# The weights of the seven products, moved by 96 bytes inside their tiles

## The chip, the core and the metric

The kernel runs on one core of a Trainium2 chip. The metric is the time of one execution on the device in microseconds (us). The core has a matrix engine (TensorE, PE in the profile, with its weight loads as PEld), a vector engine (VectorE, DVE), a scalar engine (ScalarE, ACT), GpSimd (POOL) and a queue that starts transfers (SyncE, SP). Operands of TensorE lie in SBUF, a memory of 128 partitions; an address here is a byte position inside a partition, the same in all 128.

## The reference

A trunk of two layers on 512 frames of 1024 features, float32. Layer 0 has multi-head latent attention, layer 1 chunked attention with a learned bias on one shared key and value; both have a SwiGLU feed-forward part of width 2816, and a norm before and after each part.

```python
def swiglu(h, w_gate, w_up, w_down):
    return (jax.nn.silu(h @ w_gate) * (h @ w_up)) @ w_down

for layer in range(DEPTH):                       # 2
    h = rms_norm(x, attn_pre_g[layer])
    y = mla_mixer(h, ...) if layer < N_A_LAYERS else chunked_mixer(h, ...)
    x = x + rms_norm(y, attn_post_g[layer])
    h = rms_norm(x, ffn_pre_g[layer])
    f = swiglu(h, ffn_w_gate[layer], ffn_w_up[layer], ffn_w_down[layer])
    x = x + rms_norm(f, ffn_post_g[layer])
```

The change touches `h @ w_gate` and `h @ w_up` alone.

## The kernel before

Every float32 matrix product is made of three matmuls. Weights and activations are each split into a high part (rounded to the matmul's format fp32r) and a low part (what is left), and high x high, low x high and high x low are added up in PSUM. A class `Feed` brings the weights: a transfer of 128 x 1024 floats into a `raw` tile, a cast on ScalarE into `whi` (line 141), and a subtraction on VectorE into `wlo` (line 142). `whi` and `wlo` have three buffers each in the pool `wp`, 4096 bytes a partition. `Feed.split` (lines 210 to 239) takes the tiles and hands out a function `at`, from which the matmuls get their 128-column pieces.

Of the 22 blocks of 128 hidden columns, 4 are done whole with matmuls of 512 columns (lines 257 to 260); the other 18 go in 9 pairs a layer through `products` (lines 1038 to 1084). There the 2 x 2 block product of (gate, up) weights with two halves of the activations is made with seven products in place of eight, from sums of weights and of activations. The class `Pair` loads the four blocks of weights of a pair and forms the sums on VectorE (line 171); such weights are those of the plan whose `src` is a `Pair`. One pair is 7 products x 2 output blocks x 4 steps of the contraction x 3 = 168 matmuls at line 1064, each with 128 x 128 weights (`whi` or `wlo`) and 256 moving columns (`th`, `tl`, `xh`, `xl`). They add into PSUM tiles `be`, `al` and `ga`, in the order be, al, ga, al, al, al, be; so the chain shows 48, 24, 24 and 72 in a row. ScalarE and VectorE take the results out (lines 1068 to 1083). Each of the seven weights is used for 24 matmuls.

Where things lie: the pools follow each other in SBUF, and tiles in them without gaps. The small constants end so that all large tiles start at 64 past a multiple of 128 bytes, and even at 192 past a multiple of 512; pieces are cut at multiples of 512 bytes. So in each fp32r matmul of the kernel before, weights and moving operand start at the same place of a 512-byte stretch. Exceptions are the identity (at 0 past a multiple of 128), which is the moving operand of the transposes, and single columns of small tiles of 32 bytes, which line 371 spreads over 128 columns and which start at many multiples of 4.

Of the kernel before, what the change touches and what calls it, by code (L numbers as in the profile page):

```python
# [11 lines left out]
F32R = mybir.dt.float32r  # L12
# [6 lines left out]
D, S, P = 1024, 512, 128  # L19
# [49 lines left out]
def trunk(ctx: ExitStack, tc: tile.TileContext, a, out):  # L69
# [4 lines left out]
    wp = ctx.enter_context(tc.tile_pool(name="wp", bufs=1))  # L74
# [7 lines left out]
    def name_(n):  # L82
        uid[0] += 1
        return f"{n}_{uid[0]}"

    def U(dt=F32, name="u"):
        return up.tile([P, S], dt, tag="u", name=name_(name), bufs=NU)
# [52 lines left out]
    def split(dst_hi, dst_lo, src):  # L140
        return (nc.scalar.copy(dst_hi, src),  # L141
                V.tensor_tensor(dst_lo, src, dst_hi.bitcast(F32), op=OP.subtract))  # L142
# [41 lines left out]
    class Feed:  # L184
# [25 lines left out]
        def split(self, i):  # L210
            while len(self.ready) <= min(i, len(self.plan) - 1):
                j = len(self.ready)
                self.load(j + 2)
                raw, (src, n, gain, room) = self.raw[j], self.plan[j]
                for f in range(j, min(j + 5, len(self.plan))):
                    self.load(f) if isinstance(self.plan[f][0], Pair) else None
                if isinstance(src, Pair):
                    src.sums(gain)
                    raw = src.raw[gain]
                elif gain is not None:  # L220
                    rv = raw[:, :n].rearrange("p (a b) -> p a b", a=gain.shape[1])
                    V.tensor_tensor(rv, rv, gain, op=OP.mult)
                if room is None:
                    pieces = [tuple(wp.tile([P, 1024], F32R, tag=t, name=name_("w" + t), bufs=3) for t in ("hi", "lo"))]
                else:
                    pieces = self.room[room]()
                w = pieces[0][0].shape[1]
                for c in range(0, n, w):
                    m = min(w, n - c)
                    with ExitStack() as st:  # L230
                        for b in self.behind.get(j, ()):
                            st.enter_context(tc.issue_after(b.ins))
                        split(pieces[c // w][0][:, :m], pieces[c // w][1][:, :m], raw[:, c:c + m])

                def at(c, m, pieces=pieces, w=w):
                    o = c % w
                    return tuple(t[:, o:o + m] for t in pieces[c // w])

                self.ready.append(at)
# [142 lines left out]
    class Head:  # L382
# [19 lines left out]
        def turn(self, qt):  # L402
            if self.pt is None:
                self.pt = [pool[0].tile([P, NQT, S], F32R, tag=t, name=name_(t), bufs=n)
                           for t, n in (("pth", 2), ("ptl", 1))]
            n = P * (qt + 1)
            p = self.p.pop(qt)
            t = bank("t", "pt")
            for kt in range(qt + 1):
                nc.tensor.transpose(t[:, kt * P:(kt + 1) * P], p[:, kt * P:(kt + 1) * P], ident)  # L410
            tv = t[:, :n].rearrange("p (a b) -> p a b", b=P)
            q_ = slice(qt * P, (qt + 1) * P)
            split(self.pt[0][:, :qt + 1, q_], self.pt[1][:, :qt + 1, q_], tv)
# [154 lines left out]
    class Split:  # L568
# [5 lines left out]
        def each(self, k, h):  # L574
            c = HALF[h]
            if len(self.xs) <= k:
                self.xs.append((U(F32R, "xh"), U(F32R, "xl")))
            t = cut(self.xs[k], c)
            if self.gain is None:
                split(*t, self.x[k][:, c])  # L580
            else:
                split_scaled(*t, self.x[k][:, c], g(self.gain, k))
# [87 lines left out]
    for k in range(KT):  # L670
        h, l = U(F32R, "xh"), U(F32R, "xl")
        w = feed.next(384, False)
# [14 lines left out]
    for j in range(2):  # L687
        t = U(name="ckv")
# [49 lines left out]
    for j in range(2):  # L738
        V.tensor_tensor(ckv[j], ckv[j], rkv, op=OP.mult)
        h, l = U(F32R, "ckh"), U(F32R, "ckl")  # L740
        feed.behind[13] = feed.behind[14] = split(h, l, ckv[j])
        cks.append((h, l))
# [484 lines left out]
    for kc in range(4):  # L1227
        w = feed.next(1024)
# [111 lines left out]
```

## Time and profile before

| | |
|---|---|
| median of 3 runs | 1162.41 us (1161.83 to 1162.87) |
| the profiled execution | 1162.01 us, span from first to last instruction 1159.9 us |
| TensorE matmuls | busy 98% of the span |
| VectorE | busy 71% |
| ScalarE | busy 53% |
| granted TensorE clock, mean | 0.997 of full speed |

Busy times of matmuls overlap, since a matmul is recorded from its start to the end of its results; their pace is read from the distance of their starts. A time line rounds starts to 0.01 us.

### The profile page before, as it was taken

How to read it: one execution, taken by the hardware profiler on the slowest of the kernel's cores; microseconds unless marked ns; L12 is line 12 of the kernel's file. 1: busy time of each engine (PE TensorE's matmuls, PEld its weight loads, DVE VectorE, ACT ScalarE, POOL GpSimd, SP SyncE). 2: the span in 40 equal slices, each digit the busy share in tenths (PEclk: the TensorE clock that was granted, in tenths of full speed). 3: DMA queues.
4: the chain of work that ended last, by engine and by line, in shares of the span. 5: the costliest groups of instructions: out<-in, count | busy, mean ns of one | idle time of the engine just before them, and what ended most of it. 6: DMA issues, size and time to landing. Idle time of an engine off the chain costs nothing.

```text
span 1159.9 us, 18693 instructions
## 1 busy us (share of the span) xinstructions
PE 1137.9 (98%) x7195; PEld 1018.7 (88%) x7195; DVE 828.8 (71%) x1429; ACT 613.9 (53%) x1159; POOL 29.5 (3%) x51
## 2 busy tenths in 40 slices
PE   9999999999999999999999999999999999999996
PEld 6788889899999998889788887789899999998886
DVE  7787648999898862246968877748998998852233
ACT  6476646656565542224436766656655565632220
POOL 1200000000000000000100000000000000000002
PEclk9999999999999999999999999999999999999998
DMA  7333144323333253233456656454223233252212
GB/s 231 117 113 91 37 149 160 109 79 105 109 92 127 74 170 103 96 118 96 159 158 159 172 152 164 128 176 138 87 92 114 90 108 109 73 189 89 91 50 73
DMA packets 53161, 137.71 MB, mean 119 GB/s; under 512 B 7184, under 2 KB 10768, under 8 KB 53072
## 3 DMA queue, kind: packets, MB, share of 16 engines
q1 hardware_dynamic: 52928, 136.47, 37.6%
q8 instruction: 57, 0.93, 0.3%
q14 instruction: 32, 0.26, 0.1%
q10 hardware_dynamic: 144, 0.04, 0.0%
HBM read 113.22 MB, written 8.59 MB: 105 GB/s over the span
## 4 chain that ended last, share of the span: by engine, by line
PE 85%; DVE 7%; ACT 3%; issue 2%; DMA 2%; POOL 1%; SPq 0%; DVEq 0%; ACTq 0%; POOLq 0%
PE al L1064 16%; PE b L258 16%; PE b L259 16%; PE b L260 16%; PE be L1064 8%; PE ga L1064 4%; PE pt L410 2%; DVE wlo L142 1%; DVE acc L328 1%; POOL r L354 1%; DMA raw<-in_w_pair 1%; ACT whi L141 1%; PE b L1189 1%; PE bc L371 1%; PE b L1190 1%
## 5 line engine op out<-in xcount | busy, mean ns | idle before, releaser
L142 DVE TENSOR_TENSOR wlo<-raw,whi 128x1024 fp32r<-128x1024 f32 (+4 forms) x240 | 278.8, 1162 | 199.0 <-ACT whi L141 197.3
L141 ACT CAST whi<-raw 128x1024 fp32r<-128x1024 f32 (+4 forms) x240 | 240.7, 1003 | 337.8 <-PE b L259 180.6
L258 PE MATMUL b<-hh,whi 128*128 128x512 f32 (+1 forms) x364 | 136.0, 374 | 0.0
L259 PE MATMUL b<-hl,whi 128*128 128x512 f32 (+1 forms) x364 | 135.7, 373 | 0.0
L260 PE MATMUL b<-hh,wlo 128*128 128x512 f32 (+1 forms) x364 | 135.6, 373 | 0.0
L1064 PE MATMUL al<-th,whi 128*128 128x256 f32 x432 | 124.2, 288 | 0.6 <-DVE ut L1076 0.3
L1064 PE MATMUL al<-tl,whi 128*128 128x256 f32 x432 | 122.1, 283 | 0.0
L1064 PE MATMUL al<-th,wlo 128*128 128x256 f32 x432 | 122.1, 283 | 0.0
L258 PE MATMUL b<-xh,whi 128*128 128x512 f32 (+1 forms) x304 | 115.7, 383 | 0.8 <-ACT xh L145 0.8
L259 PE MATMUL b<-xl,whi 128*128 128x512 f32 (+1 forms) x304 | 113.1, 372 | 0.0
L260 PE MATMUL b<-xh,wlo 128*128 128x512 f32 (+1 forms) x304 | 112.8, 371 | 0.0
L171 DVE TENSOR_TENSOR raw<-raw,raw 128x1024 f32<-128x1024 f32 x72 | 86.6, 1218 | 1.1 <-DMA raw<-in_w_pair 0.9
L1064 PEld LDWEIGHTS al<-th,whi 128*128 128x128 f32 x432 | 82.7, 191 | 2.9 <-DVE ut L1076 0.8
L1064 PEld LDWEIGHTS al<-th,wlo 128*128 128x128 f32 x432 | 82.7, 192 | 0.0
L1064 PEld LDWEIGHTS al<-tl,whi 128*128 128x128 f32 x432 | 82.7, 191 | 0.0
L259 PEld LDWEIGHTS b<-hl,whi 128*128 128x128 f32 x364 | 68.5, 188 | 12.0
L258 PEld LDWEIGHTS b<-hh,whi 128*128 128x128 f32 x364 | 68.5, 188 | 12.0
L260 PEld LDWEIGHTS b<-hh,wlo 128*128 128x128 f32 x364 | 68.5, 188 | 11.9
L398 ACT ACTIVATE p<-p,mn 128x128 f32<-128x128 f32 (+1 forms) x96 | 54.0, 562 | 31.9 <-DVE mn L396 31.2
L142 DVE TENSOR_TENSOR ptl<-pt,pth 128x128 fp32r<-128x128 f32 (+1 forms) x96 | 46.3, 485 | 28.8 <-ACT pth L141 23.0
L328 DVE TENSOR_TENSOR acc<-acc,sq 128x256 f32<-128x256 f32 (+1 forms) x89 | 43.3, 505 | 32.1 <-ACT sq L327 31.3
L258 PEld LDWEIGHTS b<-xh,whi 128*128 128x128 f32 x304 | 57.4, 189 | 9.0 <-ACT xh L145 2.1
(266 smaller groups left out, 2831.0 us busy)
## 6 DMA issues: line engine op xcount, KB each, us to landing
raw<-in_w_pair SPq DMA_DIRECT2D x72, 512.0 KB, 3.8
raw<-in_w_down SPq DMA_DIRECT2D x38, 512.0 KB, 3.4
raw<-in_w_o SPq DMA_DIRECT2D x16, 512.0 KB, 3.6
raw<-in_w_gu SPq DMA_DIRECT2D x16, 512.0 KB, 3.7
raw<-in_w_qkb SPq DMA_DIRECT2D x16, 512.0 KB, 3.6
x<-in_x SPq DMA_DIRECT2D x16, 256.0 KB, 5.8
mid<-x SPq DMA_DIRECT2D x16, 256.0 KB, 2.2
x<-mid SPq DMA_DIRECT2D x16, 256.0 KB, 6.2
```

The source lines that it names most:

```text
L141: return (nc.scalar.copy(dst_hi, src), V.tensor_tensor(dst_lo, src, dst_hi.bitcast(F32), op=OP.subtract))
L142: V.tensor_tensor(dst_lo, src, dst_hi.bitcast(F32), op=OP.subtract))
L171: V.tensor_tensor(t, x, y, op=OP.add)
L258: nc.tensor.matmul(o, l[0], r[0], start=start, stop=False)
L259: nc.tensor.matmul(o, l[0], r[1], start=False, stop=False)
L260: nc.tensor.matmul(o, l[1], r[0], start=False, stop=stop)
L328: V.tensor_tensor(self.acc[:, c], self.acc[:, c], q[:, c], op=OP.add)
L354: nc.gpsimd.tensor_tensor(r, v, mhalf[:, :m], op=OP.pow)
L371: nc.tensor.transpose(b[:, (first + i) * P:(first + i + 1) * P], col[:, i:i + 1].to_broadcast([P, P]), ident)
L398: nc.scalar.activation(p[:, :n], p[:, :n], AF.Exp, bias=mn[:, :1], scale=-1.0, accum_out=self.sums[:, qt:qt + 1])
L410: nc.tensor.transpose(t[:, kt * P:(kt + 1) * P], p[:, kt * P:(kt + 1) * P], ident)
L1064: nc.tensor.matmul(o, l[c], r[d], start=first_ and n == 0, stop=k == K2 - 1 and n == 2, skip_group_check=True)
```

## The change

Tiles `whi` and `wlo` get 1056 in place of 1024 elements, 4224 bytes. For weights of a `Pair` the slice that is written and read begins at element 24, that is at byte 96, and 64 + 96 = 160 is 32 past a multiple of 128. All other weights begin at byte 0 of the wider tile.

```diff
@@ -221,7 +221,9 @@
                 if room is None:
-                    pieces = [tuple(wp.tile([P, 1024], F32R, tag=t, name=name_("w" + t), bufs=3) for t in ("hi", "lo"))]
+                    o = 24 if isinstance(src, Pair) else 0
+                    pieces = [tuple(wp.tile([P, 1056], F32R, tag=t, name=name_("w" + t), bufs=3)[:, o:o + 1024]
+                                    for t in ("hi", "lo"))]
                 else:
                     pieces = self.room[room]()
```

The lists of instructions of all engines stay the same, row for row. 3024 of the matmuls, all at line 1064, have their weights at 32 past a multiple of 128 afterwards and their moving operand at 64, as before. All other operands stay where they were past a multiple of 128. Counted from a multiple of 512 more moves: buffers of `whi` and `wlo` are now 4224 bytes apart, and the pools behind `wp` (the small tiles and the tiles of each attention and feed-forward part) begin 768 bytes later.

## Rows read from the trace of the kernel before

**Rows 1.** Page, parts 1 and 2: busy time and share; TensorE's clock.
```profile
PE 1137.9 (98%) x7195; PEld 1018.7 (88%) x7195; DVE 828.8 (71%) x1429; ACT 613.9 (53%) x1159; POOL 29.5 (3%) x51
...
PEclk9999999999999999999999999999999999999998
```

**Rows 2.** Page, part 4: the chain that ended last, by line.
```profile
PE al L1064 16%; PE b L258 16%; PE b L259 16%; PE b L260 16%; PE be L1064 8%; PE ga L1064 4%; PE pt L410 2%; DVE wlo L142 1%; DVE acc L328 1%; POOL r L354 1%; DMA raw<-in_w_pair 1%; ACT whi L141 1%; PE b L1189 1%; PE bc L371 1%; PE b L1190 1%
```

**Rows 3.** The chain in order of time, product stages: start, duration in us, what.
```profile
254.77 1.70 PE al L1064 x12
...
262.24 2.88 PE al L1064 x24
...
419.22 2.88 PE be L1064 x24
...
861.07 1.70 PE al L1064 x12
...
1025.22 2.88 PE be L1064 x24
```

**Rows 4.** Windows of both product stages, line 1064 alone: length, busy (instructions).
```profile
254.77:422.10 167.33, 167.13 (x1380) 166.02 (x1380) 1.00 0.30 97
861.07:1028.10 167.03, 167.03 (x1380) 166.02 (x1380) 1.00 0.31 97
```

**Rows 5.** Time line in a product: start, duration in us, engine, line, instruction.
```profile
270.11 0.28 PE L1064 MATMUL al<-tl,whi 128*128 128x256 f32 x1
270.12 0.19 PEld L1064 LDWEIGHTS al<-th,wlo 128*128 128x128 f32 x1
270.23 0.28 PE L1064 MATMUL al<-th,wlo 128*128 128x256 f32 x1
...
270.35 0.28 PE L1064 MATMUL al<-th,whi 128*128 128x256 f32 x1
270.36 0.19 PEld L1064 LDWEIGHTS al<-tl,whi 128*128 128x128 f32 x1
270.47 0.28 PE L1064 MATMUL al<-tl,whi 128*128 128x256 f32 x1
```

**Rows 6.** Time line in the down projection, 512 moving columns; between them two matmuls.
```profile
500.17 0.39 PE L258 MATMUL b<-hh,whi 128*128 128x512 f32 x1
...
500.85 0.39 PE L258 MATMUL b<-hh,whi 128*128 128x512 f32 x1
```

**Rows 7.** Line 371's loads (min/median/max ns), then the time line behind its last.
```profile
L371 PEld LDWEIGHTS bc<-ident,r x32: 132/136/138, 30.5 to 1151.4; 128*128 128x128 f32 x32
...
31.24 0.14 PEld L371 LDWEIGHTS bc<-ident,r 128*128 128x128 f32 x1
...
31.35 0.19 PEld L258 LDWEIGHTS b<-xh,whi 128*128 128x128 f32 x1
...
31.46 0.19 PEld L259 LDWEIGHTS b<-xl,whi 128*128 128x128 f32 x1
```

**Rows 8.** One pair: window (PE, PEld, DVE, ACT busy); groups of splits in it.
```profile
322.00:342.31 20.31, 20.31 (x171) 20.21 (x170) 18.32 (x24) 11.92 (x20) 0.00 (x0) 1.00 0.34 104
...
L142 DVE TENSOR_TENSOR wlo<-raw,whi 128x1024 fp32r<-128x1024 f32 x7 | 8.6, 1221 | 2.0 <-ACT whi L141 2.0
...
L141 ACT CAST whi<-raw 128x1024 fp32r<-128x1024 f32 x7 | 7.4, 1050 | 6.8 <-PE al L1064 3.6 <-PE be L1064 1.8 <-issue 1.4
```

**Rows 9.** Time line in the attention of layer 1, 512 columns; some matmuls left out.
```profile
611.25 0.40 PE L258 MATMUL b<-xh,whi 128*128 128x512 f32 x1
...
611.48 0.40 PE L259 MATMUL b<-xl,whi 128*128 128x512 f32 x1
611.48 0.19 PEld L260 LDWEIGHTS b<-xh,wlo 128*128 128x128 f32 x1
...
611.72 0.39 PE L260 MATMUL b<-xh,wlo 128*128 128x512 f32 x1
...
612.41 0.39 PE L260 MATMUL b<-xh,wlo 128*128 128x512 f32 x1
```

## The prediction

> **What bounds the kernel now.** I read the page first, then the chain that ended last, then the matmuls one by one. TensorE is busy for 1137.9 of 1159.9 us, and its clock row holds nines to the last slice but one: it runs at the higher of its two levels, 2.4 GHz [rows 1]. The chain spends 16% of the span on the `al` products, 8% on `be` and 4% on `ga`, together 28%, and next to nothing on VectorE, ScalarE or DMA [rows 2]. So the pace of the matmuls sets the time, and the change touches only the matmuls of line 1064.
>
> There are 2 layers x 9 pairs x 168 = 3024 of these. In the chain they run from 254.77 to 422.10 us in layer 0 and from 861.07 to 1028.10 us in layer 1 [rows 3], 334.4 us in all. The view by windows shows PE busy 334.16 of 334.36 us in them [rows 4]. The stage waits for nobody; only a change of the matmul's own pace can shorten it.
>
> That pace: in the run without a wait, matmul starts stand at 270.11, 270.23, 270.35, 270.47 us, so 0.120 us each, and 24 in a row take 2.88 us [rows 3, 5]. The weight loads stand just behind them, at 270.12 and 270.36 us: the load for the next matmul begins when the present one begins, so weights and moving columns are read at the same time. Compare 512 columns: from 500.17 to 500.85 us three matmuls pass, 0.2267 us each [rows 6]. The difference, 0.1067 us for 256 more columns, is 0.417 ns a column, one column per cycle at 2.4 GHz. Hence 256 columns alone would take 106.7 ns, and each matmul, short or long, carries 13.3 ns beyond its columns. The whole question is what these 13.3 ns are: over 3024 products they make 40 us.
>
> **The change part by part.** No instruction is added, removed or moved; every engine has the same list in the same order, the same waits, the same DMAs. Three things differ, all of them addresses.
>
> (1) The products' weights are read from 32 past a multiple of 128 instead of 64, while the moving operand stays at 64. The trace of before can't price this directly: there both operands of all these fp32r matmuls start at the same place of a 128-byte stretch. I bound it. Below: weight loads of the identity transposes, which have the shortest matmuls, follow each other in 0.11 us (31.24, 31.35, 31.46 us) [rows 7]. So at best the pace falls from 120 to 110 ns, 3024 x 10 ns = 30 us. VectorE sets nearly the same floor: in one pair it is busy 18.32 of 20.31 us [rows 8], so not more than 2.0 us a pair, 36 us over 18 pairs, could come out. Above: the same 512-column matmul also runs slower than 226.7 ns. After two score matmuls of another length, six of them start from 611.25 to 612.41 us, five steps of 0.232 us, though the loads stand beside the matmuls as before (the one at 611.48 us, too) [rows 9]; single steps there are 0.24. That is +5 ns (the mean) to some +10 ns (a step of 0.24, 0.01 us above 0.23), so +16 to +30 us over 3024.
>
> What speaks for a value between these ends? The nearest rows on the address of stationary operands are the loads of line 371. Their sources are single columns of small tiles that lie at many places (0, 4, 32, 36, 64, 72, 96, 100 and others past a multiple of 128), and 32 of them took 132 to 138 ns [rows 7]; no place stands out. They read one word again and again, 128 times, and run beside 128 columns that lie at 0, so they are a weak witness. Then there are the 13.3 ns themselves, equal at 256 and 512 columns: a price per matmul, as a swap of weights would be, or as one more stretch of the moving operand would be, fits without any help of the weights' address. I take 0 for this term, and keep -30 and +30 us for the range.
>
> The Trainium skill has a rule that bears on it: "TensorE: Matmul & The Clock Gate", section "Step-by-step: what each phase is for", says that TensorE reads moving and stationary operands through two independent ports, and that loading the next weights takes no read bandwidth from the running matmul. By it this term is 0 whatever the addresses, and the time stays. The 0.232 us of [rows 9], with the same columns and the same loads as the 0.2267, are not explained by it, so I do not rest on it.
>
> (2) ScalarE and VectorE write the high and low parts to the shifted place: 7 casts of 1050 ns and 7 subtractions of 1221 ns a pair [rows 8]. No row has such a write elsewhere. It is hidden: VectorE idles 20.31 - 18.32 = 2.0 us a pair and ScalarE 8.4 us, and three buffers of each tag let the split run ahead of the matmuls. A write dearer by 10% would add 7 x 0.12 = 0.85 us a pair, within the 2.0. Without that cover it would cost 18 x 0.85 = 15 us. I take 0. The first split of each stage lies ahead of the first product without such cover, two times 0.1 us at most.
>
> (3) The padded tiles push the other weights in these buffers, and the pools behind them, by multiples of 128 bytes. These operands stay at 64 past a multiple of 128. If a coarser stretch than 128 bytes mattered, the 512-column matmuls would feel it too; no row shows or excludes that. I take 0, and let the same two bounds stand for it.
>
> Sum: 0. The profiled execution took 1162.0 us for a span of 1159.9, with 2.1 us around it; the median of the runs is 1162.4. Forecast 1162.4.
>
> **The rivals.**
> *The change does nothing measurable* (my forecast): 1162.4, within 0.2%, which is about 2.3 us and what a measurement of this kernel can tell from no change. For it: the constant excess at both lengths, whichever of `th`, `tl`, `xh`, `xl` moves and whether `whi` or `wlo` is loaded; and that the stage runs in perfect step.
>
> *The two reads disturb each other less.* If the 13.3 ns come from the load and the stream getting in each other's way because both begin at the same place of a 128-byte stretch at the same moment, a shift by 32 bytes can relieve that. For it: loads and matmuls start within 0.01 us of each other in every row [rows 5], and the excess is not strictly fixed [rows 9]. Against it: the stream moves twice as fast as the load (512 bytes of weights in 110 ns, 1024 of columns in 107), so it passes the load's place again and again whatever the start. The best is -30 us, 1132; half of it, taken as the middle of nothing and all, is -15 us, 1147. Below 18.3 us a pair VectorE would be the new bound.
>
> *The two reads disturb each other more.* The lock in which the products run, 120.0 ns again and again, is broken, and they run as the 512-column matmuls do at 611 us: +5.3 ns each, 1162.4 + 16 = 1178, up to 1192. It decides as soon as a product takes over 0.8 ns more than now, since 3024 x 0.8 ns is 2.4 us. For it: [rows 9] show that such a slower step exists with nothing late. Against it: those rows are a stream just disturbed, and the down projection settles at 226.7.
>
> *A new wait on VectorE or ScalarE*, because writes at the shifted place are dear: up to 15 us by part (2) if they grew by far more than 10%. I give it a few in a hundred and count it with slower.
>
> That the shift doesn't take place is no rival: the offset of 24 elements is added to the slice that both the split and the matmuls use.
>
> **How the numbers follow.** I give no measurable effect 0.40, less disturbance 0.36, more disturbance (with the new wait) 0.24. The explanations of the excess that leave the weights' address out are simplest, but the trace holds no fp32r product with the two operands at different places, so it doesn't weaken the other two much; and of these I hold the gain for somewhat likelier, since both operands beginning together looks more like an unlucky place than a lucky one. Predicted time: 1162.4, its own range 1160 to 1165. The range for 8 in 10 reaches to 1140 below, which leaves out about 0.12 of gains above three quarters of the bound, and to 1178 above, which leaves out some 0.08.
>
> **What the profile of the changed kernel would show.** Right: products still 0.12 us apart, 2.88 us for 24, a pair at 20.31 us; stages of 167 us; splits at 1050 and 1221 ns. Wrong towards faster: 24 products in 2.6 to 2.8 us, and VectorE above 18.3 of a shorter pair, perhaps with waits for `wlo`. Wrong towards slower: 24 products in 3.0 us, or starts that no longer repeat. If the stages keep their length but the down projection (0.2267 us a step) changes, part (3) was the mistake. If `wlo` or `whi` takes longer and PE waits for it, part (2) was.

## The result and the profile after

The changed kernel takes 1165.14 us (median of 12 runs, 1163.81 to 1166.31) against 1162.45 us (12 runs): ratio 1.0022, interval 1.0013 to 1.0030. It is slower by 2.7 us, 0.22%, and that is more than its measurement is uncertain. The forecast was no measurable change, 1162.4 us, with 1160 to 1165 as its own range.

That small sum hides two larger parts of opposite sign. First the page after: its busy times, and the chain by line.

```profile
span 1164.3 us, 18693 instructions
...
PE 1140.8 (98%) x7195; PEld 1014.9 (87%) x7195; DVE 828.9 (71%) x1429; ACT 614.2 (53%) x1159; POOL 29.5 (3%) x51
...
PE b L261 16%; PE al L1066 16%; PE b L260 16%; PE b L262 16%; PE be L1066 8%; PE ga L1066 4%; PE pt L412 2%; DVE wlo L142 2%; DVE acc L330 1%; ACT whi L141 1%; POOL r L356 1%; DMA raw<-in_w_pair 1%; PE bc L373 1%; PE b L1191 1%; PE b L1192 1%
```

The page looks the same as before; the shift is below its percentages. (Lines past 224 are two further down: line 1066 is the products, 260 to 262 the other matmuls.) The chain in order of time shows the first part: start, duration, what.

```profile
256.16 1.69 PE al L1066 x12
257.85 5.67 PE be L1066 x48
263.52 2.86 PE al L1066 x24
266.38 2.84 PE ga L1066 x24
269.22 8.67 PE al L1066 x72
...
865.14 1.68 PE al L1066 x12
...
1027.06 2.84 PE be L1066 x24
```

Groups of 24 products take 2.84 to 2.86 us where [rows 3] had 2.88. So the products became faster. The stretch of [rows 3] now runs in layer 1 from 865.14 to 1029.90, 164.8 in place of 167.0 us. (The stretches of [rows 3] hold 2 x 1380 of the 3024 products; each stage begins some 16 us earlier, with products that wait in between. The two whole stages took 183.4 and 183.3 us, now 181.1 and 180.9, so -4.7 us.)

The second part is in the down projection, whose weights were not given the offset. Time line after, line 260 to 262, 512 moving columns:

```profile
469.84 0.39 PE L260 MATMUL b<-hh,whi 128*128 128x512 f32 x1
470.06 0.40 PE L261 MATMUL b<-hl,whi 128*128 128x512 f32 x1
470.30 0.40 PE L262 MATMUL b<-hh,wlo 128*128 128x512 f32 x1
470.53 0.39 PE L260 MATMUL b<-hh,whi 128*128 128x512 f32 x1
470.76 0.40 PE L261 MATMUL b<-hl,whi 128*128 128x512 f32 x1
470.99 0.40 PE L262 MATMUL b<-hh,wlo 128*128 128x512 f32 x1
471.23 0.39 PE L260 MATMUL b<-hh,whi 128*128 128x512 f32 x1
```

Six matmuls take 1.39 us, 0.232 us each; in [rows 6] it was 0.2267. In the unrounded starts most groups of three have one step of about 0.227 and two of 0.233 and 0.234.

To add this up I took from the traces the distance from each matmul's start to the next start, wherever it is less than the time of the columns at one per 2.4 GHz cycle plus 32 ns in both traces (longer ones were left out as waits). The products' mean went from 119.92 to 118.16 ns; that of the 924 matmuls of 512 columns in the down projection from 226.73 to 231.94 ns, +4.8 us; that of the some 1260 others of 512 columns from 229.25 to 231.69 ns, +3.1 us. With -4.7 us from the product stages that is +3.2. A wait for a transfer in the attention of layer 1, 0.9 us, and small ones make the rest of the 4.4 us by which the span grew. This execution, 1166.31 us, is the slowest of the 12, so the medians differ by less.

The splits didn't change. Groups of one pair after (320 to 340.1 us):

```profile
L142 DVE TENSOR_TENSOR wlo<-raw,whi 128x1024 fp32r<-128x1024 f32 x8 | 9.8, 1220 | 1.7 <-ACT whi L141 1.6
...
L141 ACT CAST whi<-raw 128x1024 fp32r<-128x1024 f32 x7 | 7.4, 1052 | 6.5 <-PE al L1066 3.6 <-PE be L1066 1.5 <-issue 1.4
```

1220 and 1052 ns stand against 1221 and 1050 in [rows 8]: writing to the other place costs nothing here.

### The profile page after: what moved, and what is told of

It reads as the page before. It is cut to its first block, busy times and chain, and to the rows that moved or that the text cites. A ratio compares the mean times of both kernels' runs of the same rounds, so it can differ in the third digit from the quotient of the medians.

```text
span 1164.3 us, 18693 instructions
## 1 busy us (share of the span) xinstructions
PE 1140.8 (98%) x7195; PEld 1014.9 (87%) x7195; DVE 828.9 (71%) x1429; ACT 614.2 (53%) x1159; POOL 29.5 (3%) x51
## 4 chain that ended last, share of the span: by engine, by line
PE 84%; DVE 8%; ACT 3%; issue 2%; DMA 2%; POOL 1%; SPq 0%; ACTq 0%; DVEq 0%; POOLq 0%
PE b L261 16%; PE al L1066 16%; PE b L260 16%; PE b L262 16%; PE be L1066 8%; PE ga L1066 4%; PE pt L412 2%; DVE wlo L142 2%; DVE acc L330 1%; ACT whi L141 1%; POOL r L356 1%; DMA raw<-in_w_pair 1%; PE bc L373 1%; PE b L1191 1%; PE b L1192 1%
## 5 line engine op out<-in xcount | busy, mean ns | idle before, releaser
L141 ACT CAST whi<-raw 128x1024 fp32r<-128x1024 f32 (+4 forms) x240 | 240.6, 1003 | 340.1 <-PE b L261 185.7
L262 PE MATMUL b<-hh,wlo 128*128 128x512 f32 (+1 forms) x364 | 138.1, 379 | 0.0
```

What stands on the lines that cost most here:

```text
L141: return (nc.scalar.copy(dst_hi, src), V.tensor_tensor(dst_lo, src, dst_hi.bitcast(F32), op=OP.subtract))
L262: nc.tensor.matmul(o, l[1], r[0], start=False, stop=stop)
```

## The experiments

Two theories at first. **Theory A**: the weights of the next matmul are loaded while the present one reads its moving columns, and the pace depends on where the two start against each other in some stretch of addresses. **Theory B**: it depends on whether successive loads start alike. The rows above fit both: with buffers 4224 bytes apart, some of the high and low buffers now differ by 128 bytes from each other and from the moving operands. In the expectations below, theory A first counts places in 128 bytes, as the change's own words do, and in later runs in 256.

All paces, worked out from the traces as above, in ns (products; 512 columns in the down projection; other matmuls of 512 columns). The place is that of the loaded weights minus that of the moving operand, past a multiple of 256 bytes:

| kernel | place: products | place: others | products | down | other 512 |
|---|---|---|---|---|---|
| before | 0 | 0 | 119.92 | 226.73 | 229.25 |
| the change | 96 and 224 | 0 and 128 | 118.16 | 231.94 | 231.69 |
| e1_pad | 0 and 128 | 0 and 128 | 118.79 | 231.94 | 231.76 |
| e2_all96 | 96 | 96 | 117.78 | 234.27 | 233.18 |
| e3_lo128 | high 0, low 128 | the same | 119.11 | 231.17 | 231.13 |
| e4_all128 | 128 | 128 | 118.68 | 232.37 | 232.20 |
| e5_both | 96 and 224 | 0 | 118.23 | 226.74 | 229.28 |
| e6_all256 | 0 (256 further) | 0 (256 further) | 119.92 | 226.73 | 229.34 |
| e7_all64 | 64 | 64 | 114.68 | 233.32 | 232.88 |
| e8_all32 | 32 | 32 | 118.32 | 233.34 | 232.69 |
| e9_only64 | 64 | 0 | 114.74 | 226.73 | 229.37 |
| e10_only192 | 192 | 0 | 117.78 | 226.69 | 229.36 |
| e11_shift | 0 (all operands 64 further) | 0 | 119.92 | 226.73 | 229.14 |
| e12_only16 | 16 | 0 | 118.32 | 226.77 | 229.30 |

**e1_pad: the wide tiles without the offset.**

```diff
-                    pieces = [tuple(wp.tile([P, 1024], F32R, tag=t, name=name_("w" + t), bufs=3) for t in ("hi", "lo"))]
+                    pieces = [tuple(wp.tile([P, 1056], F32R, tag=t, name=name_("w" + t), bufs=3)[:, :1024]
+                                    for t in ("hi", "lo"))]
```

> The wider tiles alone: 4224 bytes each, but all weights begin at byte 0, so the products' weights stay at 64 past a multiple of 128. Theory A (a matmul's pace follows from where the weights loaded beside it lie against its moving operand, counted in 128 bytes): the products return to 120 ns, the matmuls of 512 columns stay as slow as in the changed kernel (231.8 ns in the mean, +7.9 us), so about 1170 us. Theory B (the pace follows from whether successive weight loads begin at the same place of some longer stretch; if all are alike the stream locks at 13.3 ns beyond its columns, wherever they lie): buffers still differ by 128 bytes, so the products run near 118 ns as in the changed kernel, the rest too, and the time is about 1165 us.

1167.14 us against 1162.63, ratio 1.0039 (1.0026 to 1.0051). The matmuls of 512 columns are as slow as in the changed kernel, 231.94 ns: the padding does that, not the offset. The products stay near 119: theory A in 128 bytes had them back at 120 and the time at 1170, theory B at 118 and 1165, and neither is met. A distance of 128 bytes is no harmless one. The offset itself, the change against this kernel, is worth 118.79 - 118.16 = 0.6 ns a product, 1.9 us: it lowers the price of the padding.

**e2_all96, e3_lo128, e4_all128: tiles of 4096 bytes, but gaps of unused bytes ahead of, between and behind the high and low buffers.**

```diff
+    def gap(tag, n):
+        if n and tag not in gone:
+            gone.add(tag)
+            wp.tile([P, n], F32, tag=tag, name=name_("gap"), bufs=1)
...
-                    pieces = [tuple(wp.tile([P, 1024], F32R, tag=t, name=name_("w" + t), bufs=3) for t in ("hi", "lo"))]
+                    pieces = [(gap("ga", A) or tile_w("hi"), gap("gb", B) or tile_w("lo"))]
+                    gap("gc", C)
```

A, B, C in elements are 24, 0, 104; then 0, 32, 96; then 32, 0, 96. What lies behind keeps its place in a stretch of 512 bytes.

> Tiles of 4096 bytes as before, but a gap of 96 bytes ahead of the buffers of high and low parts and one of 416 bytes behind them: all weights that pass through these buffers, the products' and the others, begin at 288 past a multiple of 512, everything else at 192 as before. Theory A: the products run at about 118 ns as in the changed kernel (-5 us), since their place against the moving operand is the same, and the matmuls of 512 columns move one way or the other: 1157 us if these keep their pace. Theory B: all loads are alike again, so 120.0 and 226.7 ns everywhere and 1162.4 us.

> Tiles of 4096 bytes, with 128 bytes between the high and the low buffers and 384 behind them: high parts at 192 past a multiple of 512 as before, low parts at 320, all else as before. Theory B: in each group of three matmuls the load changes place twice, so the down projection shows the cycle 227, 233, 234 ns of the changed kernel, the products run near 118 to 119 ns, and the time is about 1165 us, though no operand has left 64 past a multiple of 128. Theory A counted in 128 bytes: nothing changes, 1162.4 us. Theory A counted in 256 or 512 bytes: only the matmul beside which a low part is loaded is slower, 227, 233, 227, about 1163 to 1165 us.

> Tiles of 4096 bytes, a gap of 128 bytes ahead of the high and low buffers, 384 behind them: all these weights at 320 past a multiple of 512, their moving operands at 192. Theory A counted in 256 or 512 bytes: each load lies 128 bytes away from the moving operand, as in the slow steps of the changed kernel, so matmuls of 512 columns run at 232 to 234 ns: +10 to +15 us, 1172 to 1177 us. Theory B: all loads are alike, 120.0 and 226.7 ns, 1162.4 us.

e2: 1168.06 us, 1.0047 (1.0035 to 1.0060). e3: 1166.36, 1.0033 (1.0021 to 1.0046). e4: 1167.42, 1.0045 (1.0032 to 1.0057). In e2 and e4 all loads start alike, and theory B asked for 120.0 and 226.7 ns; it measured 117.8 and 234.3, 118.7 and 232.4. Theory B falls. Theory A in 128 bytes falls with e3 and e4, where nothing should have changed. In 256 or 512 bytes it had the down projection of e4 rightly at 232 to 234 ns; the time stayed some 5 us below the lower end of the expected 1172 to 1177, since the products gained and the matmuls of 512 columns ran at the lower end. In e2, with every load at the same place, the down projection runs like this:

```profile
472.10 0.40 PE L269 MATMUL b<-hh,whi 128*128 128x512 f32 x1
472.33 0.40 PE L270 MATMUL b<-hl,whi 128*128 128x512 f32 x1
472.56 0.39 PE L271 MATMUL b<-hh,wlo 128*128 128x512 f32 x1
472.80 0.39 PE L269 MATMUL b<-hh,whi 128*128 128x512 f32 x1
473.03 0.40 PE L270 MATMUL b<-hl,whi 128*128 128x512 f32 x1
473.27 0.40 PE L271 MATMUL b<-hh,wlo 128*128 128x512 f32 x1
```

Five steps take 1.17 us, 0.234 each, and nothing waits in between. e3 goes against theory A in part. Counted in 256 bytes it had 227, 233, 227 ns and 1163 to 1165 us; the cycle came as theory B had it, and the time is 1166.4. Time line of e3:

```profile
472.13 0.40 PE L270 MATMUL b<-hl,whi 128*128 128x512 f32 x1
472.36 0.40 PE L271 MATMUL b<-hh,wlo 128*128 128x512 f32 x1
472.60 0.39 PE L269 MATMUL b<-hh,whi 128*128 128x512 f32 x1
472.82 0.40 PE L270 MATMUL b<-hl,whi 128*128 128x512 f32 x1
```

In the mean over the down projection, a step whose own weights and whose loaded weights both lie at the equal place takes 226.9 ns. The step beside which a low part is loaded takes 232.4 ns. The next one, which uses that low part, takes 234.2 ns though a high part at the equal place is loaded beside it. So one load at another place is followed by two slow steps. Theory A is right in that the place counts, and wrong in that only the matmul beside the load pays; why the second one does is open.

**e5_both: the products as in the change, the other weights put back against their moving operands.**

```diff
-                    o = 24 if isinstance(src, Pair) else 0
+                    i = next(turn)
...
-                                    for t in ("hi", "lo"))]
+                                    for t, o in (("hi", 24 if isinstance(src, Pair) else (0, 32, 0)[i]),
+                                                 ("lo", 24 if isinstance(src, Pair) else (32, 0, 32)[i])))]
...
+    slots = "021" * 9 + "012" * 31 + "010" + "210" * 8 + "120" * 31
+    turn = map(int, slots)
```

`turn` says which of the three buffers comes next. In this kernel some instructions also stand in another order: three matmuls in the first stage, and a tenth or so of the places in the lists of ScalarE and VectorE.

> The changed kernel, with the products' weights at byte 96 as there, but every other weight moved by 0 or 128 bytes inside its wide tile, by a table of the buffers' order, so that it starts at 192 past a multiple of 256, as its moving operand does. Theory A, counted in 256 bytes (the pace follows from the place of the loaded weights against the moving operand; equal places lock at 13.3 ns beyond the columns): the products keep 118.2 ns (-5 us), the matmuls of 512 columns are back at 226.7 ns, and the time is about 1157.5 us. If the stretch is 512 bytes: the down projection stays slow (its moving operands are at 448 past a multiple of 512), about 1162 us. Theory C (the products are faster only because successive loads vary): also 1157 us; this run doesn't tell A from C.

1160.41 us against 1162.69, 0.9981 (0.9972 to 0.9990): faster than both kernels. The down projection is back at 226.74 ns though its moving operands lie at 448 past a multiple of 512 and part of the weights at 192, so the stretch is 256 bytes, not 512. Theory C had fallen with e2 already, where all loads start alike and the products run at 117.8 ns. The paces of e5 are as expected, the time is 3 us above it. Its profiled execution loses 3.3 us in the first 16 us of the kernel against the profile of before. TensorE idles there for 2.62 us ahead of 10.10 us, waiting for `xh` (0.79 us before), and from 11.2 to 14.6 us its granted clock is 0.5, the 1.2 GHz level, with 0.43 us a matmul in place of 0.23. The two product stages give -4.1 in place of -5. Whether the other runs lose at the start as well is not shown.

**e6_all256, e7_all64, e8_all32: gaps as in e2**, of 64, 16 and 8 elements ahead (256, 64 and 32 bytes) and 64, 112 and 120 behind.

> Tiles of 4096 bytes, all high and low parts 256 bytes further (448 past a multiple of 512), everything else as before. Theory A counted in 256 bytes: nothing changes, 120.0 and 226.7 ns, 1162.4 us. Counted in 512 bytes: as with 128 bytes, down projection at 232 ns or more and products near 118 to 119, 1167 us.

> As before, all high and low parts 64 bytes further. Theory A, graded: with 96 bytes products ran at 117.8 and the down projection at 234.3 ns, with 128 bytes at 118.7 and 232.4; 64 bytes give some third pair of numbers. Theory A, in which any place but the equal one is alike: products 118 to 119, down projection 232 to 234, about 1167 us.

> As before, all high and low parts 32 bytes further. If the lock needs exactly equal places: 118 to 119 and 232 to 234 ns, about 1167 us. If it only needs the places to lie within some tens of bytes: 120.0 and 226.7 ns, 1162.4 us.

e6: 1162.76 us, 1.0000 (0.9991 to 1.0009), 119.92 and 226.73 ns: 256 bytes are like none. e8, a single run: 1167.7 us, 118.3 and 233.3 ns; 32 bytes already end the equality. e7, a single run: 1160.9 us, where one form of theory A had 1167, and a surprise. The products at 64 bytes, time line of e7:

```profile
301.80 0.28 PE L1075 MATMUL be<-th,whi 128*128 128x256 f32 x1
301.91 0.28 PE L1075 MATMUL be<-tl,whi 128*128 128x256 f32 x1
302.02 0.28 PE L1075 MATMUL be<-th,wlo 128*128 128x256 f32 x1
302.14 0.28 PE L1075 MATMUL be<-th,whi 128*128 128x256 f32 x1
302.25 0.28 PE L1075 MATMUL be<-tl,whi 128*128 128x256 f32 x1
302.37 0.28 PE L1075 MATMUL be<-th,wlo 128*128 128x256 f32 x1
302.48 0.28 PE L1075 MATMUL be<-th,whi 128*128 128x256 f32 x1
302.59 0.28 PE L1075 MATMUL be<-tl,whi 128*128 128x256 f32 x1
```

Seven steps in 0.79 us: 113 ns each, again a stream in step, with 6.7 ns beyond the 106.7 of its columns, half of the 13.3. The matmuls of 512 columns pay as at the other places (233.3 ns). Matmuls of 256 columns in other stages gain, too: those with weights from the same buffers take 115.3 to 118.1 ns by groups (119.2 to 120.0 before), while those with weights from other tiles (`wh`, `wu`) stay at 119.3 to 120.1 ns in every run.

**e9_only64, e10_only192: 64 bytes further, or 64 bytes less (192), for the products alone.** Tiles of 4352 bytes keep all buffers alike past a multiple of 256.

```diff
-                    pieces = [tuple(wp.tile([P, 1024], F32R, tag=t, name=name_("w" + t), bufs=3) for t in ("hi", "lo"))]
+                    o = 16 if isinstance(src, Pair) else 0
+                    pieces = [tuple(wp.tile([P, 1088], F32R, tag=t, name=name_("w" + t), bufs=3)[:, o:o + 1024]
+                                    for t in ("hi", "lo"))]
...
-    nc = bacc.Bacc("TRN2", target_bir_lowering=False, num_devices=1, dynamic_dma_scratch_size=1024)
+    nc = bacc.Bacc("TRN2", target_bir_lowering=False, num_devices=1, dynamic_dma_scratch_size=768)
```

In e10 the 16 is a 48.

> Tiles of 4352 bytes (17 times 256), so that all buffers keep the same place in a stretch of 256 bytes; the products' weights begin at byte 64, all others at byte 0; the memory for it comes from a scratch area made 256 bytes smaller. Theory A (places counted in 256 bytes, equal places lock at 13.3 ns beyond the columns, +64 locks products at 6.7 ns): products at 113.3 to 114.7 ns as with all weights at +64 (-15 us in the stream, some 4 us given back to waits for VectorE), matmuls of 512 columns at 226.7 ns in the down projection, time about 1150 to 1152 us. If the rival that the products only gain from what the other matmuls do beside them (order of buffers, waits) were right, they would fall back to 118 to 120 ns and the time would be 1157 to 1162 us.

> The same with the products' weights at byte 192, that is 64 bytes before the place of the moving operand instead of behind it. If only the distance counts: 113 to 115 ns and about 1151 us. If the side counts, as a race of two reads at different speeds would have it: another pace, between 115 and 122 ns, 1155 to 1165 us.

e9: 1155.75 us against 1162.3, 0.9945 (0.9932 to 0.9959), the fastest of all. Products 114.74, down projection 226.73 ns, as expected; the products do not fall back to 118 to 120, so the rival in its expectation is out. The time lies 4 us above the expected 1150 to 1152. Its five runs spread from 1150.39 to 1157.82 us, more than those of the other kernels. The chain of the profiled (and fastest) run shows what bounds it:

```profile
268.10 8.55 PE al L1066 x72
276.64 5.44 PE be L1066 x48
282.08 2.72 PE al L1066 x24
284.80 2.72 PE ga L1066 x24
287.52 2.73 PE al L1066 x24
...
290.49 1.06 ACT whi L141
...
291.57 1.23 DVE wlo L142
...
293.05 1.22 DVE raw L171
...
307.99 4.63 DMA raw<-in_w_pair
```

24 products take 2.72 us, 113.3 ns each. But from 290 us the chain passes through the split, the sums and a transfer: the weights now come late. The window from 269.91 to 287.52 us of this kernel (PE, PEld, DVE, ACT busy) shows how full VectorE is:

```profile
269.91:287.52 17.61, 17.61 (x154) 17.40 (x154) 16.43 (x21) 10.43 (x18) 0.00 (x0) 1.00 0.28 93
```

VectorE is busy 16.43 of 17.61 us, 93%, where it was 90% in [rows 8]. A supply that runs without room turns each late transfer into waiting, which may be why the runs spread; that was not tried.

e10, a single run: 1157.0 us, products 117.78 ns. The side counts: +64 and -64 are not the same.

**e11_shift: everything moved together by 64 bytes.**

```diff
+    consts.tile([P, 16], F32, name="gap")
```

> The kernel before with a gap of 64 bytes behind the constants, so that all large tiles, weights and moving operands alike, begin at a multiple of 256; their place against each other stays equal. In all runs so far the moving operands lay at 192 past a multiple of 256, so the place of the weights alone (their address) and their place against the moving operand could not be told apart. Theory A (against the moving operand): equal places lock at 13.3 ns, 120.0 and 226.7 ns, 1162.4 us. Theory D (the address of the weights alone): weights at 0 past a multiple of 256, as with +64 before, so products near 114 ns and the down projection at 233 ns, about 1161 us in sum, by the paces plainly different.

1161.77 us, 0.9992 (0.9983 to 1.0002); 119.92 and 226.73 ns. In all runs before this one the moving operands lay at one place, so the address of the weights alone could have been the cause. Here the weights lie where e7 and e9 have them, at 0 past a multiple of 256, and the products take their old 2.88 us for 24. Time line of e11's chain:

```profile
262.00 2.88 PE al L1066 x24
264.88 2.88 PE ga L1066 x24
267.76 8.79 PE al L1066 x72
```

So the address of the weights alone does not decide. In e11 every large tile moved, though, and in the other runs the moving operand of these streams kept its place. The traces hold the opposite case as well: in the value projections (lines 779 and 1102) tiles `whi` and `wlo` are the moving operand, and the loaded weights (`ckh`, `xh` and their low parts) lie in a pool ahead of them, which stays where it was in e2. Time lines of before, then of e2:

```profile
597.86 0.39 PE L258 MATMUL b<-whi,xh 128*128 128x512 f32 x1
...
599.90 0.39 PE L258 MATMUL b<-whi,xh 128*128 128x512 f32 x1
```

```profile
601.64 0.39 PE L269 MATMUL b<-whi,xh 128*128 128x512 f32 x1
...
603.75 0.39 PE L269 MATMUL b<-whi,xh 128*128 128x512 f32 x1
```

Nine steps take 2.04 us before and 2.11 in e2. The mean of these streams (183 steps) is 233.4 ns in e2, 232.9 in e4, 232.6 in e7 and 233.3 in e8, against 227.0 to 227.1 before, in e6 and in e11. Moving the weights alone changes the pace, so does moving the moving operand alone, and moving both by the same distance doesn't: the place of the two against each other decides.

**e12_only16: the products' weights 16 bytes further** (o = 4 in e9).

> As the kernel with only the products' weights at +64, but with these at +16 bytes. If the lock needs equal places to the byte or to 16 bytes: products leave 120.0 ns, near 118. If it only needs the same 32-byte stretch: 120.0 ns and 1162 us.

A single run: 1158.3 us, products at 118.32 ns. 16 bytes suffice to leave the 120.0.

## Why the prediction was wrong

**What held.** The chain was read rightly: the pace of the matmuls sets the time, the product stages follow it, the granted clock of the stages stayed, and waits took back only 0.5 us there (5.2 us gained in the stream, 4.7 in the stages). Part (2), the splits at the new place, is 0 as forecast, 1220 and 1052 ns.

**Part (1), the products, taken as 0.** It measured -1.8 ns a matmul and -4.7 us in the two stages. The bounds held it (-30 to +30). The step of this part that failed is the reading of the 13.3 ns as a price for each matmul "as a swap of weights would be, or as one more stretch of the moving operand would be". Equal excess at 256 and 512 columns was no witness for that: the load lasts as long in both. With the loaded weights 64 bytes off, half of the excess goes where the stream is in step (e7, e9); moving both by the same 64 bytes leaves it whole (e11). The loads of line 371, at many addresses, were indeed a weak witness, for the address of the weights alone doesn't matter. I wrote that the trace holds no fp32r product with the two operands at different places; that should have weighed more than it did. The rows of the lower bound are misread, though the bound stands: of the three loads in [rows 7] only the first is a transpose's (line 371), the next two are those of lines 258 and 259; loads of transposes do follow each other in 108 to 110 ns elsewhere in that trace.

**Part (3), the other weights, taken as 0.** This step failed and made the kernel slower: +4.8 us in the down projection and +3.1 us in the other matmuls of 512 columns, where 0 was taken with no row for it. The working had said ahead of it that the change touches only the matmuls of line 1064; by its padding it touches all that use these buffers. The step said that operands which stay at 64 past a multiple of 128 stay as they were. The stretch that counts is 256 bytes (e4 against e6, and e5), and buffers 4224 bytes apart alternate between two places in it. The lines that it speaks of have 48% of the chain in [rows 2], more than the products. The sign at which the profile would show it, a change of the down projection, was named and came true, beside a change of the stages.

**The rivals.** In pace, both happened at once, each in other matmuls: the products became faster, the matmuls of 512 columns slower. That the time came within 3 us of the forecast is luck: two terms that were taken as 0 measured -4.7 and +7.9 us. The slower rival's price, the 0.232 us of [rows 9], is also the pace of the down projection after; that is a coincidence as far as is shown, since in [rows 9] both operands lie at equal places. And it was laid on the products, where the stream of 256 columns gains at all unequal places tried, 1 to 5 ns.

**The rule.** The Trainium skill, "TensorE: Matmul & The Clock Gate", section "Step-by-step: what each phase is for", has the load of the next weights take no read bandwidth from the running matmul, through a port of its own. The prediction drew from it that the addresses cannot matter. This case's runs disagree with that: the same instructions take 119.9, 118.3, 117.8 or 114.7 ns by nothing but the place of the weights that are loaded beside them. Whether it is read bandwidth that is lost, no run shows.

**What stays open.** Why streams of 256 columns gain and those of 512 lose when the places differ; why +64 falls into step at 113.3 ns and -64 doesn't; what in the memory has the length of 256 bytes; why in e3 the step after an unequal load is slow as well; why the other matmuls of 512 columns take 229.25 ns in the mean, and 0.232 us in [rows 9], though their places are equal. That the two reads get in each other's way is argued and not shown. Other offsets than 16, 32, 64, 96, 128 and 192 bytes (and 224, mixed with 96, in the change) were not tried, and none was found at which 512 columns run faster than at equal places.

## What to carry to other kernels

Before an allocation is changed, write down for each group of matmuls where its loaded weights and its moving operand start past a multiple of 256 bytes; a pad that is meant for one group moves the others. With fp32r weights that are loaded anew for each matmul, start from equal places for 512-column streams, and try 64 bytes for 256-column ones: here that alone gave 0.55%. A page whose shares stay the same can hide two effects of 5 to 8 us, so compare the distances of starts, group by group.

## What was not expected of the hardware

Addresses in SBUF change the pace of matmuls that wait for nothing: 113.3 to 120.0 ns for 256 columns and 226.7 to 234.3 ns for 512, at the same granted clock (1.00, the 2.4 GHz level). Equal places past a multiple of 256 bytes give a stream in strict step in the products and the down projection, 120.0 and 226.7 ns; 16 bytes of difference end that for the products, 32 for both. And a faster TensorE was at once bound by VectorE and by transfers: in e9's profiled run, the fastest of five, waits in the product stages gave back about 3 of 15 us, and in the median e9 is only 6.55 us faster than the kernel before.
